# A transformer block on one core: differential queries and keys projected with the tokens stationary, attention pieces and transposing moves at other places

## Chip, cores and metric

One NeuronCore of a Trainium2 chip runs the whole program. The metric is the device time of one execution in microseconds, taken as the median of several runs. A profile of one execution lies beside it; its own time differs a little from the median.

## What is computed

The input is 256 tokens of width 2048 in fp32. Two blocks follow each other: one with sliding-window attention, then one with two attention branches (MLA and differential) whose results are gated and added, and a feed-forward network (FFN). The change lies mostly in the differential branch. Of its projection `dq` and `dk` are 2048 wide each: 8 heads, in each of them two queries and two keys of 128.

```python
S, D, HEADS, HEAD_DIM = 256, 2048, 8, 128

def diff_branch(dq, dk, dv, lq1, lk1, lq2, lk2, sub_g, lambda_init, slopes):
    q = dq.reshape(b, s, DIFF_HEADS, 2, DIFF_HEAD_DIM)
    k = dk.reshape(b, s, DIFF_HEADS, 2, DIFF_HEAD_DIM)
    v = dv.reshape(b, s, DIFF_HEADS, DIFF_V)
    ...
        sc = jnp.einsum('bqhmd,bkhmd->bhmqk', qb, k).astype(jnp.float32) * scale
        sc = sc + alibi[None, :, None]
        sc = jnp.where(chunk_allowed(q_pos, k_pos)[None, None], sc, NEG_INF)
        p = jax.nn.softmax(sc, axis=-1)
        a = (p[:, :, 0] - lam * p[:, :, 1]).astype(v.dtype)
        return jnp.einsum('bhqk,bkhd->bqhd', a, v)
    ...
    o = rmsnorm_2(o, sub_g) * (1.0 - lambda_init)

def second_block(x, ...):
        h = rmsnorm_2(x, attn_norm_g[i])
        c_q, c_kv, k_pe, dq, dk, dv, gate_logits = jnp.split(h @ w_in[i], split_at, axis=-1)
        y_mla = mla_branch(...)
        y_diff = diff_branch(dq, dk, dv, ...)
        g = jax.nn.sigmoid(gate_logits + b_gate[i]).reshape(b, s, 2, d)
        merged = g[:, :, 0] * (y_mla @ w_mla_proj[i]) + g[:, :, 1] * (y_diff @ w_diff_proj[i])
        x = x + merged @ w_out[i]
        h2 = rmsnorm_2(x, ffn_norm_g[i])
        x = x + (jax.nn.silu(h2 @ w_ffn_gate[i]) * (h2 @ w_ffn_up[i])) @ w_ffn_down[i]
    return rmsnorm_2(x, final_norm_g)
```

## The kernel before

**Weights.** All projections together are 5440 weight tiles of 128x128 fp32, used once each. `W.load` (L54) fetches them in chunks of 16 tiles (1 MB) on SP's queue into four buffers `w_raw`. `W.cut` halves a chunk into two cuts of 8 tiles: ACT casts a cut to `w_hi` (L85, rounded fp32), DVE subtracts to `w_lo` (L86); four cuts are held. With activations split in the same way, each tile costs three products.

**Two forms of a projection.** `gemm` holds the weight tile stationary and moves the activations (features on partitions in the result): per tile one matmul with 512 columns (`w_hi` with both parts of the activations) and one with 256 (`w_lo` with the high part). `gemm_nat` holds 128 tokens stationary and moves four weight tiles at once: per four tiles six matmuls with 512 columns, results with tokens on partitions. A strip is 512 columns of output, 64 tiles. `gemm_nats` runs several strips half by half: the first `late` rows of tiles of each, then the rest of each; before, the out projection and the first two strips of the FFN use it.

**Turning.** A result with tokens on partitions is turned by `turned` (L456): DVE transposes it in 32x32 blocks, and `moved` (L444) issues 16 small DMAs that put the blocks where they belong. All 16 go to one queue, POOL's if nothing else is said, or every fourth to another (`fourth`).

**What sets the order.** The projections are written one after another; attention and turning are generators that `between` steps after every few tiles (8 in this stretch, 16 later), at most `apart` ticks from each other; `yield n` in one means that it goes on n ticks later. `between.drain()` finishes what is left. Each engine executes its instructions in order, so a waiting instruction holds up everything behind it on its engine, casts of weights and loads among them.

**The stretch that changes.** For u = 0..3 (two heads each) the main loop projects 4 feature blocks of `dq` and 4 of `dk` with `gemm` (ACT copies half of PSUM to `qk_d`, L417; DVE adds the other half and multiplies, L212), then a strip `dv` with `gemm_nat` (`v_hi`, L984), then queues `attend_d` (L914): `probs_d` for two heads (scores, softmax), `turned_probs` (L462, every fourth move on SP), `values_d` (L885: `a_hi` at L889 needs the turned probabilities), `turned_values` (L903), and the output's split. In u = 0 follow four gates, the MLA projections, and `turn_residual` (L961), which turns the residual stream to `x1n`, 128 moves, all on SP. After the loop come four more gates, a drain, four strips of the diff projection whose merged results are turned, then the out projection and the FFN, whose products are turned and split by `split_turned` (L471: waits 5 ticks, then ACT's `t_hi` at L480). Block 2's MLA heads run as `attend_m` (L787).

## Time and profile before

| | us |
|---|---|
| median of 3 runs | 1979.8 |
| lowest, highest | 1979.0, 1981.18 |
| the profiled execution | 1978.53 |
| its span, first to last instruction | 1976.8 |
| TensorE (PE) busy in it | 1961.3 |
| VectorE (DVE) / ScalarE (ACT) / GpSimd (POOL) busy | 1246.6 / 1000.3 / 524.8 |

PE is TensorE, SP the engine that issues loads. Durations below are of the profiled execution. Instructions on PE overlap at their ends, so a matmul's listed duration is longer than the distance to the next one's start; the distance is what counts.

### The profile page before, as it was taken

Reading aid. Unit: us, or ns where it says so; the run is one execution under the profiler, and the core shown is the slowest. Engines: PE = TensorE matmul, PEld = TensorE weight load, DVE = VectorE, ACT = ScalarE, POOL = GpSimd, SP = SyncE. Lnnn points to the kernel's source line nnn. Section 1 sums busy time; section 2 is a strip of 40 time slices with the busy share of each in tenths; the row PEclk is TensorE's granted clock in tenths of the full one; section 3 lists DMA queues with packets and bytes.
Section 4 is the critical chain, followed back from the end, with each engine's and each line's share of the span. In section 5 each row is a group of like instructions: output and inputs, shape, how many; then the busy total and the mean of one; then the engine's idle time right before and its main releaser. Section 6 shows DMA issues by size and latency. Waiting matters only on the chain. (4 is left out here: it accounts for less than half of the span.)

```text
span 1976.8 us, 27209 instructions
## 1 busy us (share of the span) xinstructions
PE 1961.3 (99%) x9756; PEld 1648.6 (83%) x9756; DVE 1246.6 (63%) x1960; ACT 1000.3 (51%) x1580; POOL 524.8 (27%) x1067
## 2 busy tenths in 40 slices
PE   9999999999999999999999999999999999999998
PEld 8888888888888888888888888887888888888887
DVE  7889766888856655566666666655555555545553
ACT  6677664755645444455554444544444444444443
POOL 0555200022401300013143575433444333330000
PEclk9999999999999999999999999999999999999999
DMA  8565554455555555555556665655656556565553
GB/s 304 186 210 192 187 208 164 171 177 175 174 187 195 173 220 226 198 182 181 204 202 228 212 216 186 241 204 199 207 206 206 204 208 210 206 226 192 192 191 107
DMA packets 100793, 393.16 MB, mean 199 GB/s; under 512 B 27248, under 2 KB 53104, under 8 KB 57520
## 3 DMA queue, kind: packets, MB, share of 16 engines
q1 hardware_dynamic: 65184, 366.17, 52.1%
q0 software_dynamic: 34320, 23.27, 4.2%
q10 hardware_dynamic: 1152, 1.97, 0.3%
q8 instruction: 77, 1.26, 0.3%
q14 instruction: 60, 0.49, 0.1%
HBM read 364.03 MB, written 2.10 MB: 185 GB/s over the span
## 5 line engine op out<-in xcount | busy, mean ns | idle before, releaser
L86 DVE TENSOR_TENSOR w_lo<-w_raw,w_hi 128x1024 fp32r<-128x1024 f32 (+1 forms) x677 | 820.8, 1217 | 555.6 <-ACT w_hi L85 550.7
L85 ACT CAST w_hi<-w_raw 128x1024 fp32r<-128x1024 f32 (+1 forms) x677 | 706.6, 1048 | 699.4 <-PE ps_g L209 632.1
L209 PE MATMUL ps_g<-w_lo,t_hi 128*128 128x512 f32 x1176 | 457.6, 389 | 0.8 <-DVE w_lo L86 0.8
L209 PE MATMUL ps_g<-w_hi,t_hi 128*128 128x512 f32 x1176 | 457.6, 389 | 0.3 <-ACT w_hi L85 0.3
L209 PE MATMUL ps_g<-w_hi,t_lo 128*128 128x512 f32 x1176 | 457.3, 389 | 0.0
L452 POOL DMA_DIRECT2D turned<-turn x576 | 281.7, 497 | 393.2 <-DVE turn L459 169.6
L209 PE MATMUL ps_g<-h,w_hi 128*128 128x512 f32 x1160 | 283.7, 393 | 1.9 <-ACT w_hi L85 1.8
L452 POOL DMA_DIRECT2D prob_t<-prob_tr x336 | 164.5, 498 | 400.6 <-DVE prob_tr L467 249.6
L209 PEld LDWEIGHTS ps_g<-w_lo,t_hi 128*128 128x128 f32 x1176 | 220.7, 188 | 47.0 <-DVE w_lo L86 1.1
L209 PEld LDWEIGHTS ps_g<-w_hi,t_hi 128*128 128x128 f32 x1176 | 220.7, 188 | 46.7 <-ACT w_hi L85 0.7
L209 PEld LDWEIGHTS ps_g<-w_hi,t_lo 128*128 128x128 f32 x1176 | 220.7, 188 | 45.6
L209 PEld LDWEIGHTS ps_g<-h,w_hi 128*128 128x128 f32 x1160 | 212.0, 188 | 46.6 <-issue 2.7
L209 PE MATMUL ps_g<-w_hi,h 128*128 128x512 f32 x768 | 240.9, 391 | 0.0
L209 PEld LDWEIGHTS ps_g<-w_hi,h 128*128 128x128 f32 x768 | 144.2, 188 | 29.8
L209 PEld LDWEIGHTS ps_g<-h,w_lo 128*128 128x128 f32 x1160 | 150.2, 191 | 9.9 <-issue 3.0
L209 PE MATMUL ps_g<-h,w_lo 128*128 128x256 f32 x1160 | 155.1, 284 | 0.0
L209 PE MATMUL ps_g<-w_lo,h 128*128 128x512 f32 x384 | 149.7, 390 | 0.8 <-DVE w_lo L86 0.8
L290 POOL TENSOR_TENSOR rstd<-ms,mhalf 128x2 f32<-128x2 f32 (+1 forms) x10 | 8.4, 837 | 354.5 <-DVE ms L285 338.8
L209 PEld LDWEIGHTS ps_g<-w_lo,h 128*128 128x128 f32 x384 | 72.1, 188 | 16.2 <-DVE w_lo L86 1.6
L452 POOL DMA_DIRECT2D o_t<-o_tr x128 | 62.8, 498 | 63.5 <-issue 24.9
L209 PE MATMUL ps_g<-w_hi,y_m 128*128 128x512 f32 x256 | 79.5, 389 | 0.0
L209 PE MATMUL ps_g<-w_hi,y_d 128*128 128x512 f32 x256 | 79.0, 389 | 0.0
(242 smaller groups left out, 1800.8 us busy)
## 6 DMA issues: line engine op xcount, KB each, us to landing
w_raw<-w SPq DMA_DIRECT2D x337, 1024.0 KB, 5.0
turned<-turn POOLq DMA_DIRECT2D x576, 16.0 KB, 3.9
prob_t<-prob_tr POOLq DMA_DIRECT2D x336, 24.0 KB, 3.6
row<-rw POOLq DMA_DIRECT2D x12, 256.0 KB, 4.0
prob_t<-prob_tr SPq DMA_DIRECT2D x112, 24.0 KB, 2.9
w_raw<-w SPq DMA_DIRECT2D x5, 512.0 KB, 7.5
x1n<-turn SPq DMA_DIRECT2D x128, 16.0 KB, 1.8
o_t<-o_tr POOLq DMA_DIRECT2D x128, 16.0 KB, 3.9
```

The source lines that it names most:

```text
L85: a = nc.scalar.copy(out=hi[:, q], in_=src[:, q])
L86: b = nc.vector.tensor_tensor(out=lo[:, q], in0=src[:, q], in1=hi.bitcast(F32)[:, q], op=ALU.subtract)
L209: nc.tensor.matmul(out=o, lhsT=a, rhs=b, start=start, stop=stop, skip_group_check=True)
L290: nc.gpsimd.tensor_tensor(out=r, in0=t, in1=mhalf[:, 0:n], op=ALU.pow)
L452: (fourth if fourth and a == 3 else queue).dma_start(out=o[32 * b:32 * b + 32, a * n:a * n + n], in_=tr[32 * a:32 * a + 32, b * n:b * n + n])
```

## The change

The differential queries and keys are projected with `gemm_nat` (the columns of their weights are permuted for it): per u two strips of 64 tiles, each with two results of 128 tokens x 512 features. ACT scales each result out of PSUM (L992), and each is turned, 12 moves on POOL and 4 on SP. A new `dense_d`, the first piece of `attend_d`, copies the turned tiles to dense queries and keys on ACT, because the turned layout is not contiguous. `attend_d` is queued before `dv` for u > 0 and begins 14 ticks later, its other pieces at 1, 2, 11, 1, 1, 13, 2 ticks behind each other; `attend_m` begins 2 ticks later. The moves of `turned_values`, of the merged strips, of the FFN's products and of `x1n` are shared 12 to POOL, 4 to SP. The gates' rows are loaded on SP. Gate 4 stands between `dqk` and `dv` of u = 3, gates 5 to 7 after the loop. The first two diff strips run half by half with `gemm_nats`, which ticks until the activation tiles exist; the drain comes behind them. The FFN's products are split 7 ticks after they are moved.

```diff
--- before.py
+++ after.py
@@ -406,6 +406,8 @@
         for ks in (range(late), range(late, n)):
             for col, pp in zip(cols, banks):
                 for k in ks:
+                    while acts[k] is None:
+                        between.tick()
                     hi, lo = W.take(name, k * P, col, 4)
                     for tb in range(2):
                         nat3(pp[tb], acts[k], tb, hi, lo, k == 0, k == n - 1)
@@ -420,14 +422,6 @@
     def scaled(o, ps, rb):
         total(o, ps)
         tt(o, o, rb, ALU.mult)
-    def scores(parts, ps):
-        n = len(parts)
-        for j, (q, k) in enumerate(parts):
-            mm(ps[:, 0:P], q[:, 0:P], k[:, 0:P], j == 0, False)
-        for j, (q, k) in enumerate(parts):
-            mm(ps[:, P:384], q[:, P:S], k[:, 0:S], False, j == n - 1)
     def exps(ps, table, scale, negmax, sums, init, rows=None):
@@ -453,11 +447,11 @@
                     out=o[32 * b:32 * b + 32, a * n:a * n + n], in_=tr[32 * a:32 * a + 32, b * n:b * n + n])
         return o
-    def turned(z, queue=nc.gpsimd):
+    def turned(z, queue=nc.gpsimd, fourth=None):
         tr = unit("turn")
         nc.vector.transpose(out=tr, in_=z)
-        return moved(tr, unit("turned"), queue)
+        return moved(tr, unit("turned"), queue, fourth)
     def turned_probs(p):
@@ -468,9 +462,9 @@
         d = moved(tr, wide("prob_t"), fourth=nc.sync).rearrange("p (a e k i) -> p e k a i", a=4, e=2, k=3)
         return [d[:, e] for e in range(2)]
-    def split_turned(acts, k0, parts):
-        yield 5
+    def split_turned(acts, k0, parts, wait=5):
+        yield wait
         hls = []
         for t in parts:
             t = t.rearrange("p (a g i) -> p g a i", a=4, g=4)
@@ -786,6 +780,7 @@
     def attend_m(j, qn, qr, kn, v):
+        yield 2
         while j // 2 not in roped:
             yield
         negmax, sums, rec = sm("negmax"), sm("sums"), sm("rec")
@@ -864,7 +859,21 @@
     tab_d = unit("tab_d")[:, 0:384]
     nc.scalar.dma_start(out=tab_d, in_=cst[:, C_DD:C_DD + 384])
-    def probs_d(head, q, k):
+    def dense_d(q, k):
+        qs, ks = [], [unit("k_d") for _ in range(2)]
+        for tb in range(2):
+            t = unit("q_d")
+            nc.scalar.copy(out=t.rearrange("p (g a i) -> p g a i", a=4, g=4),
+                           in_=q[tb].rearrange("p (a g i) -> p g a i", a=4, g=4))
+            qs.append(t)
+            for e in range(2):
+                nc.scalar.copy(out=ks[e].rearrange("p (g t a i) -> p t g a i", g=2, t=2, a=4)[:, tb],
+                               in_=k[tb].rearrange("p (a g i) -> p g a i", a=4, g=4)[:, 2 * e:2 * e + 2])
+        return qs, ks
+    def probs_d(head, e, qs, ks):
         negmax, sums, rec = sm("negmax"), sm("sums"), sm("rec")
         slope = 2.0 ** -(head + 1)
         bias = unit("bias")[:, 0:384]
@@ -872,7 +881,9 @@
         p = []
         for m in range(2):
             ps = bank("s")
-            scores([(half(q, m), half(k, m))], ps)
+            qm = [q[:, (2 * e + m) * P:(2 * e + m) * P + P] for q in qs]
+            mm(ps[:, 0:P], qm[0], ks[e][:, m * S:m * S + P], True, False)
+            mm(ps[:, P:384], qm[1], half(ks[e], m), False, True)
             p.append(exps(ps, bias, scale_d, negmax[:, 2 * m:2 * m + 2], sums[:, 2 * m:2 * m + 2], BIG))
         nc.vector.reciprocal(out=rec, in_=sums)
         nc.vector.tensor_scalar(out=rec[:, 2:4], in0=rec[:, 2:4], scalar1=neglam, scalar2=None, op0=ALU.mult)
@@ -909,26 +920,29 @@
             nc.vector.tensor_scalar(out=half(o, qb), in0=half(o, qb), scalar1=r[:, qb:qb + 1], scalar2=None,
                                     op0=ALU.mult)
             nc.vector.transpose(out=to[:, qb], in_=half(o, qb).rearrange("p (d b j) -> p d b j", d=2, b=4))
-        return moved(tr, unit("o_t"))
-    def attend_d(u, q, k, v):
+        return moved(tr, unit("o_t"), fourth=nc.sync)
+    def attend_d(u, q, k, v, wait):
         heads = (2 * u, 2 * u + 1)
+        yield wait
+        qs, ks = dense_d(q, k)
+        yield 1
         p = []
         for e, head in enumerate(heads):
-            p.append(probs_d(head, q[e], k[e]))
-            yield
+            p.append(probs_d(head, e, qs, ks))
+            yield 2 - e
         pts = turned_probs(p)
-        yield 9
+        yield 11
         ms = sm("ms_d")
         os = []
         for e in range(2):
             os.append(values_d(pts[e], [(half(a, e), half(b, e)) for a, b in v], ms[:, 2 * e:2 * e + 2]))
-            yield
+            yield 1
         r = rstd(ms, S)
-        yield
+        yield 1
         ots = [turned_values(o, r[:, 2 * e:2 * e + 2]) for e, o in enumerate(os)]
         for e, head in enumerate(heads):
-            yield 8
+            yield 2 if e else 13
             ot = ots[e].rearrange("p (a d q i) -> p d q a i", a=4, d=2, q=2)
             for d in range(2):
                 y = unit(f"y_d{2 * head + d}", F32R)
@@ -942,7 +956,7 @@
     def gate(i):
-        b = row(R_GATE, i)
+        b = row(R_GATE, i, nc.sync)
         o = []
         for tb, ps in enumerate(gemm_nat("gate", i * 512, h)):
             t = unit("gate")
@@ -966,19 +980,23 @@
                     nc.vector.transpose(
                         out=tr.rearrange("p (a m j) -> p a m j", a=4, m=4)[:, :, i, :],
                         in_=x1[4 * cb + i][:, tb * P:tb * P + P].rearrange("p (a j) -> p a j", a=4))
-                x1n.append(moved(tr, unit("x1n"), nc.sync))
-    mer = []
+                x1n.append(moved(tr, unit("x1n"), fourth=nc.sync))
+    mer, gates = [], []
     for u in range(4):
         qk = []
         for c in (0, 16):
-            for i in range(4):
-                ps = gemm("dqk", c + 4 * u + i, h)
-                if i % 2 == 0:
-                    qk.append(unit("qk_d"))
-                scaled(half(qk[-1], i), ps, rb_2)
+            parts = []
+            for tb, ps in enumerate(gemm_nat("dqk", (c + 4 * u) * P, h)):
+                z = unit("qk_d")
+                nc.scalar.activation(out=z, in_=ps, func=AF.Copy, scale=r_2[:, tb:tb + 1])
+                parts.append(turned(z, fourth=nc.sync))
+            qk.append(parts)
+        v = []
+        if u:
+            between.add(attend_d(u, qk[0], qk[1], v, 14))
+        gates.extend(gate(i) for i in ((), (), (), (4,))[u])
         pp = gemm_nat("dv", u * 512, h)
-        v = []
         for tb in range(2):
             vh, vl = unit("v_hi", F32R), unit("v_lo", F32R)
             nc.scalar.activation(out=vh, in_=pp[tb], func=AF.Copy, scale=r_2[:, tb:tb + 1])
@@ -988,28 +1006,34 @@
         if u == 0:
             between.drain()
             between.every, between.apart = 8, 3
-        between.add(attend_d(u, qk[0:2], qk[2:4], v))
-        if u == 0:
+            between.add(attend_d(u, qk[0], qk[1], v, 6))
             between.add(turn_residual())
             for i in range(4):
                 mer.append(gate(i))
                 for t, ps in zip(mer[i], gemm_nat("mla", i * 512, y_m)):
                     gated(t, ps)
-    gates = [gate(4 + i) for i in range(4)]
+    gates.extend(gate(i) for i in (5, 6, 7))
+    mg = [None] * KD
+    def merge(i, pp):
+        parts = []
+        for tb, ps in enumerate(pp):
+            t = gates[i][tb]
+            gated(t, ps)
+            tt(t, t, mer[i][tb], ALU.add)
+            parts.append(turned(t, fourth=nc.sync))
+        between.add(split_turned(mg, 4 * i, parts))
+    pairs = gemm_nats("diff", [0, 512], y_d, 8)
     between.drain()
     g_ffn = [row(R_FFN, cb, nc.sync) for cb in range(4)]
     between.every, between.apart = 16, 1
-    mg = [None] * KD
-    for i in range(4):
-        parts = []
-        for tb, ps in enumerate(gemm_nat("diff", i * 512, y_d)):
-            t = gates[i][tb]
-            gated(t, ps)
-            tt(t, t, mer[i][tb], ALU.add)
-            parts.append(turned(t))
-        between.add(split_turned(mg, 4 * i, parts))
+    for i, pp in enumerate(pairs):
+        merge(i, pp)
+    for i in (2, 3):
+        merge(i, gemm_nat("diff", i * 512, y_d))
     sums3 = sm("sums3", 8)
@@ -1058,8 +1082,8 @@
             pu = gemm_nat("ffn", DFF + u * 512, h)
         for tb, ps in enumerate(pu):
             tt(parts[tb], ps, parts[tb], ALU.mult)
-            parts[tb] = turned(parts[tb])
-        between.add(split_turned(act, 4 * u, parts))
+            parts[tb] = turned(parts[tb], fourth=nc.sync)
+        between.add(split_turned(act, 4 * u, parts, 7))
     tot = sm("tot", 10)
     fgt = []
@@ -1174,7 +1198,7 @@
         "out_a": i["w_out_a"][0][pairs],
         "in_2": in_2[:, :1280],
         "kpe": np.concatenate([kpe, kpe], axis=1),
-        "dqk": in_2[:, 1344:5440],
+        "dqk": in_2[:, 1344:5440][:, _quarters(2 * D)],
         "dv": in_2[:, 5440:7488],
         "gate": in_2[:, 7488:][:, _quarters(2 * D)],
         "uq": np.concatenate([uq[:, :, :128].reshape(768, -1), uq[:, :, 128:].reshape(768, -1)], axis=1),
```

SP around `turn_residual`, with the u = 1 projection next to it; `w_raw<-w` is a weight chunk, `x1n<-turn` a move of the residual, `row<-rw` a gate's row. Before:

```order
L54 DMA w_raw<-w 128x2048 x6
L452 DMA x1n<-turn 32x128 x32
L54 DMA w_raw<-w 128x2048 x7
L452 DMA x1n<-turn 32x128 x32
L54 DMA w_raw<-w 128x2048 x18
```

and now:

```order
L54 DMA w_raw<-w 128x2048 x6
L446 DMA x1n<-turn 32x128 x4
L484 DMA row<-rw 128x512
L54 DMA w_raw<-w 128x2048
L446 DMA x1n<-turn 32x128 x4
L54 DMA w_raw<-w 128x2048 x7
L446 DMA x1n<-turn 32x128 x8
L54 DMA w_raw<-w 128x2048 x7
L446 DMA turned<-turn 32x128 x4
```

Blocks of 32 moves between weight chunks have become blocks of 4 and 8.

POOL from the values of u = 0 to the probabilities of u = 2; `turned` are here the queries and keys, `prob_t` the turned probabilities, `o_t` the turned values. Before:

```order
L452 DMA o_t<-o_tr 32x128 x32
L490 DMA row<-rw 128x512 x2
L452 DMA prob_t<-prob_tr 32x192 x12
L290 TENSOR_TENSOR rstd<-ms,mhalf 128x4
L452 DMA o_t<-o_tr 32x128 x32
L452 DMA prob_t<-prob_tr 32x192 x12
```

and now:

```order
L446 DMA o_t<-o_tr 32x128 x24
L446 DMA x1n<-turn 32x128 x72
L446 DMA turned<-turn 32x128 x72
L446 DMA prob_t<-prob_tr 32x192 x12
L446 DMA turned<-turn 32x128 x24
L290 TENSOR_TENSOR rstd<-ms,mhalf 128x4
L446 DMA o_t<-o_tr 32x128 x24
L446 DMA turned<-turn 32x128 x24
L446 DMA prob_t<-prob_tr 32x192 x12
```

The moves of `x1n` and of the queries and keys are new in this queue, the values' moves are fewer, and the probabilities stand behind queries' moves and no longer behind the values'.

ACT in the FFN, at its second product; `t_hi` is the split of a turned product, `ffn` the activation of the next strip. Before:

```order
L1055 ACTIVATE ffn<-ps_g,r_12217 128x512 x2
L85 CAST w_hi<-w_raw 128x1024 x13
L480 CAST t_hi<-turned 128x512
L85 CAST w_hi<-w_raw 128x1024 x3
L480 CAST t_hi<-turned 128x512
L1055 ACTIVATE ffn<-ps_g,r_12217 128x512 x2
```

and now:

```order
L1079 ACTIVATE ffn<-ps_g,r_12209 128x512 x2
L85 CAST w_hi<-w_raw 128x1024 x12
L474 CAST t_hi<-turned 128x512
L85 CAST w_hi<-w_raw 128x1024 x2
L474 CAST t_hi<-turned 128x512
L85 CAST w_hi<-w_raw 128x1024 x2
L1079 ACTIVATE ffn<-ps_g,r_12209 128x512 x2
```

The first split stands one cast earlier, the second two, and two casts follow it ahead of the activation.

## Rows read from the trace of the kernel before

**Rows 1.** The page's first part: busy time, share of the span and instructions of each engine.

```profile
PE 1961.3 (99%) x9756; PEld 1648.6 (83%) x9756; DVE 1246.6 (63%) x1960; ACT 1000.3 (51%) x1580; POOL 524.8 (27%) x1067
```

**Rows 2.** What PE waited for over the whole span: us in total, times, longest us.

```profile
PE ps_g L209 <- ACT w_hi L85: 2.1, 2, 1.8
PE ps_g L209 <- DVE w_lo L86: 1.9, 4, 0.8
...
PE ps_s L209 <- DVE q_n L212: 0.9, 1, 0.9
```

**Rows 3.** Windows of the span: a strip of 64 tiles with the tokens stationary, the projection of queries and keys of u = 1 (128 tiles), two FFN strips. Columns: window, us, busy us of PE, weight loads, DVE, ACT, POOL with the number of instructions, granted clock, DMA share, GB/s.

```profile
683.30:705.06 21.76, 21.76 (x97) 18.02 (x96) 10.54 (x11) 8.33 (x8) 0.54 (x1) 1.00 0.67 236
...
770.85:817.45 46.60, 44.83 (x258) 39.27 (x256) 27.03 (x33) 19.60 (x24) 0.00 (x0) 1.00 0.69 259
...
1395.00:1438.52 43.52, 43.52 (x193) 36.04 (x192) 23.12 (x22) 19.17 (x21) 15.80 (x34) 1.00 0.58 205
```

**Rows 4.** Timeline of PE in the projection of queries and keys of u = 1: start, us, instructions; the `w_lo` matmuls of two groups of 16 tiles, five groups apart.

```profile
785.86 2.08 PE L209 MATMUL ps_g<-h,w_lo 128*128 128x256 f32 x16
...
813.69 2.08 PE L209 MATMUL ps_g<-h,w_lo 128*128 128x256 f32 x16
```

**Rows 5.** Timeline of PE at four of its waits: start, us, instructions, idle time before and what ended it.

```profile
456.34 0.38 PE L209 MATMUL ps_s<-k_n,q_n 128*128 128x128 f32 x1 [0.86 <-DVE q_n L212]
...
737.47 0.61 PE L209 MATMUL ps_g<-w_hi,h 128*128 128x512 f32 x2
738.30 0.50 PE L209 MATMUL ps_g<-w_lo,h 128*128 128x512 f32 x1 [0.21 <-DVE w_lo L86]
...
1021.99 0.61 PE L209 MATMUL ps_g<-w_hi,h 128*128 128x512 f32 x2
1023.17 0.50 PE L209 MATMUL ps_g<-w_lo,h 128*128 128x512 f32 x1 [0.57 <-DVE w_lo L86]
1023.50 0.40 PE L209 MATMUL ps_g<-w_hi,h 128*128 128x512 f32 x1
...
1365.05 0.39 PE L209 MATMUL ps_g<-w_hi,t_lo 128*128 128x512 f32 x1
1365.76 0.50 PE L209 MATMUL ps_g<-w_hi,t_hi 128*128 128x512 f32 x1 [0.32 <-ACT w_hi L85]
1367.02 0.50 PE L209 MATMUL ps_g<-w_lo,t_hi 128*128 128x512 f32 x1 [0.76 <-DVE w_lo L86]
```

**Rows 6.** Timeline of SP's queue around `turn_residual`: start, us, what it issued.

```profile
709.80 20.89 SPq L452 DMA_DIRECT2D x1n<-turn  x32
730.79 15.72 SPq L54 DMA_DIRECT2D w_raw<-w  x7
751.02 20.98 SPq L452 DMA_DIRECT2D x1n<-turn  x32
772.10 8.94 SPq L54 DMA_DIRECT2D w_raw<-w  x5
```

**Rows 7.** Timeline of ACT at the waits that precede those of PE.

```profile
735.93 2.00 ACT L85 CAST w_hi<-w_raw 128x1024 fp32r<-128x1024 f32 x2 [7.86 <-DMA w_raw<-w]
...
777.25 2.00 ACT L85 CAST w_hi<-w_raw 128x1024 fp32r<-128x1024 f32 x2 [10.59 <-DMA w_raw<-w]
...
1020.39 0.51 ACT L889 CAST a_hi<-prob_t 128x384 fp32r<-128x384 f32 x1 [7.75 <-DMA row<-rw]
...
1353.95 0.62 ACT L480 CAST t_hi<-turned 128x512 fp32r<-128x512 f32 x1 [6.46 <-DMA turned<-turn]
...
1362.98 0.62 ACT L480 CAST t_hi<-turned 128x512 fp32r<-128x512 f32 x1 [5.56 <-DMA turned<-turn]
```

**Rows 8.** Timeline of POOL: the moves of the values and probabilities ahead of the wait at 1022 us, and the first and last group of the FFN's 32 moves ahead of that at 1365 us.

```profile
988.77 5.88 POOL L452 DMA_DIRECT2D o_t<-o_tr  x12 [11.73 <-DVE rec L878]
...
1008.98 3.91 POOL L452 DMA_DIRECT2D prob_t<-prob_tr  x8 [1.87 <-DMA o_t<-o_tr]
...
1337.50 1.96 POOL L452 DMA_DIRECT2D turned<-turn  x4 [23.62 <-ACT w_hi L85]
...
1354.21 4.40 POOL L452 DMA_DIRECT2D turned<-turn  x9 [1.18 <-DMA turned<-turn]
```

**Rows 9.** Groups of instructions with their shapes, from 770 to 1075 us (u = 1 to 3): count, busy us, mean ns of one, idle time before.

```profile
L212 DVE TENSOR_TENSOR qk_d<-qk_d,rb_kr 128x256 f32<-128x256 f32 x24 | 10.1, 423 | 0.7
L212 DVE TENSOR_TENSOR qk_d<-qk_d,ps_g 128x256 f32<-128x256 f32 x24 | 10.0, 419 | 26.9 <-ACT qk_d L417 26.9
L417 ACT COPY qk_d<-ps_g 128x256 f32<-128x256 f32 x24 | 8.9, 370 | 43.8 <-PE ps_g L209 43.8
...
L984 ACT ACTIVATE v_hi<-ps_g,r 128x512 fp32r<-128x512 f32 x6 | 4.1, 690 | 3.0 <-PE ps_g L209 3.0
```

**Rows 10.** The same view of the FFN's beginning, 1280 to 1420 us.

```profile
L459 DVE STREAM_TRANSPOSE turn<-ffn 128x512 f32<-128x512 f32 x6 | 4.2, 701 | 0.0
...
L480 ACT CAST t_hi<-turned 128x512 fp32r<-128x512 f32 x6 | 3.7, 620 | 18.7 <-DMA turned<-turn 18.7
```

**Rows 11.** DMA issues: queue, count, KB of each, median us from issue to landing.

```profile
turned<-turn POOLq DMA_DIRECT2D x576, 16.0 KB, 3.9
...
x1n<-turn SPq DMA_DIRECT2D x128, 16.0 KB, 1.8
```

**Rows 12.** The stretch of u = 1 to 3 as one window; columns as in rows 3.

```profile
770.85:1074.23 303.38, 301.04 (x1543) 257.73 (x1542) 190.50 (x301) 152.85 (x253) 69.98 (x139) 1.00 0.58 205
```

## Prediction

> **What bounds the kernel now.** I read the busy shares first: PE works 1961.3 us, 99% of the span, and no other engine more than 63% [rows 1]. So the time changes by two things only: what PE is given to do, and how long it stands. The list of PE's waits tells how little is left of the second: 2.1 us for ACT's casts, 1.9 us for DVE's `w_lo`, 0.9 us for `q_n` [rows 2]. The windows come next, because PE's price of a tile is in them: a strip of 64 tiles with the tokens stationary takes 21.76 us, two take 43.52 us, both at full granted clock, whereas the 128 tiles of queries and keys take 46.60 us [rows 3]. Then I followed each wait of PE in its timeline [rows 5] back to the engine and the queue that it came from [rows 6 to 8]. A gain must be in these two places; work on ACT, DVE and POOL is free as long as nobody in PE's line waits for it.
>
> **Step 1, PE's own work.** A strip of 64 tiles is 96 matmuls with 512 columns: 21.76 / 96 = 226.7 ns each, 340 ns a tile. In the old form the `w_lo` groups of five times 16 tiles start at 785.86 and 813.69 [rows 4]: 27.83 / 5 = 5.566 us for 16 tiles, 348 ns a tile. (16 matmuls of 512 are 3.63 us of that, so one of 256 columns costs 121 ns, more than half of a wide one. That surplus is what the new form avoids.) The 128 tiles of one u take 8 x 5.566 = 44.53 us now and 43.52 us after: 1.01 us, four times: **-4.0 us**. The score matmuls keep their number and shapes. A rule of the Trainium skill speaks against this step: "TensorE: Matmul & The Clock Gate", Back-to-back issue gap, gives N/2.4 + 2.5 ns for an isolated matmul, by which both forms come to about 325 ns a tile; it is a rival below.
>
> **Step 2, the waits that go.** (a) In before, SP issues the `x1n` moves in blocks of 32, which take 20.89 and 20.98 us, and the weight chunks queue behind them [rows 6]. ACT waits 7.86 and 10.59 us for `w_raw` [rows 7]. For PE the first costs 738.30 - 737.47 - 2 x 0.227 = 0.38, with 0.10 of restart (after a wait the next distance is 0.33 instead of 0.227, as at 1023.17 [rows 5]) 0.48 us; the second 46.60 - 44.53 = 2.07 us [rows 3, 4]. Now SP has at most 8 moves in a row there, 8 x 0.65 = 5.2 us, half of ACT's shorter wait, which cost 0.48. I take both as gone: -2.55 us. (b) At 1022 us ACT's `a_hi` waits 7.75 us for probabilities [rows 7] that stand on POOL behind 32 moves of values: these begin at 988.77, the probabilities' first move at 1008.98 [rows 8]. PE pays 1023.17 - 1021.99 - 0.454 + 0.10 = 0.83 us [rows 5]. The order now has queries' moves there instead (step 4). -0.83 us. From this I read ACT's cover too: 7.75 - 0.83, **6.9 us of waiting on ACT cost PE nothing**. (c) At 1365 us PE loses (1365.76 - 1365.05 - 0.227) + (1367.02 - 1365.76 - 0.227) + 0.10 = 1.61 us [rows 5], because ACT's two `t_hi` wait 6.46 and 5.56 us [rows 7] for 32 POOL moves, from 1337.50 to 1358.61, 0.66 us a move [rows 8], plus 3.9 us to land [rows 11]. With 24 moves the last lands 8 x 0.66 = 5.3 us sooner. But the second `t_hi` now stands two casts earlier, and a cast (8 tiles) is 21.76 / 8 = 2.72 us of PE, so its wait begins up to 5.4 us sooner and stays about as long; it simply ends sooner, with two casts to catch up on. So -1.61 us if ACT catches up, 0 if not; I take the gain, because ACT does a cast in 1 us [rows 7] where PE needs 2.72. (d) At 456 us PE's scores wait 0.86 us for `q_n` [rows 5]; two ticks of delay for `attend_m` are several times that: -0.9 us. Together 0.48 + 2.07 + 0.83 + 1.61 + 0.9 = **-5.9 us**.
>
> **Step 3, work that lies beside PE.** Off ACT go 32 copies of 370 ns, off DVE 64 operations of some 420 ns [rows 9]: 11.8 and 26.9 us. ACT gets 16 scalings (as `v_hi`, 690 ns [rows 9]) and 24 copies in `dense_d`, 8 of 128x512 and 16 of 128x256; the nearest rows are `t_hi`, 620 ns [rows 10], and the old copy, 370 ns [rows 9]: 11.0 + 5.0 + 5.9 = 21.9 us. DVE gets 16 transposes of 701 ns [rows 10], 11.2 us. Over 175 us of these projections that is +10 us on ACT, -16 us on DVE. ACT has 19.6 busy us in 46.6, DVE 27.0 [rows 3]: 0 on PE, with the casts' waits as the place where it would show. If a dense copy reads its strided tile twice as slowly, 11 us more over four u still lie in ACT's idle time.
>
> **Step 4, the new hand-offs.** They are not in the trace; I bound them. A pair of turned queries must be moved and landed before ACT reaches `dense_d`: 12 moves x 0.66 + 3.9 = 11.8 us for one tile, 19.7 us for two. In ACT's order eight or more casts (21.8 us) lie between the scaling and the copies, so these fit, if POOL is free. Is it? In u = 1 to 3 POOL issues 139 instructions in 303 us, 70 us busy [rows 12]; the change adds 144 moves of queries and keys and most of the 96 of `x1n`, less 24 of values. At 0.66 us that is at most (139 + 216) x 0.66 = 234 of 303 us: room, but not much. The tight place is u = 1's probabilities behind u = 2's queries: 24 + 12 moves x 0.66 + 3.9 = 27.7 us from the first scaling, where ACT's order leaves ten casts, 27.2 us. Past by 0.5 us, with 6.9 us of cover. The lower bound of all these hand-offs is 0 (cover holds); the upper, if each of two per u costs PE what the one at 1022 us did, 8 x 0.83 = 6.6 us. I take **+0.8 us**, one such wait, nearer the lower end, because the only place found short is short by 0.5 us.
>
> **The rest.** `gemm_nats` for two diff strips gives the last pieces of attention 32 more tiles of cover; PE has no wait of its own at the drain [rows 2], so 0. The gates' rows on SP cost one issue each, 0. Gate 4 is the same strip at another place, 0.
>
> **The sum.** -4.0 - 5.9 + 0.8 = -9.1 us against the profiled execution: 1978.53 - 9.1 = 1969.4. The median of the runs lies 1.27 us above that execution, so in its terms 1970.7 us, 0.46% less.
>
> **Rivals.** *The hand-offs eat the gain.* With the upper bound of step 4: 1979.8 - 9.9 + 6.6 = 1976.5 us, no change that a measurement of this kernel can tell (about 0.2%, 4 us). For it: ACT executes in order and now waits for moved tiles at 12 more places; against: the 6.9 us of cover.
> *The FFN wait stays.* Step 2(c) fails, since the splits stand earlier while their data come sooner by the same 5.3 us, and a little more is lost at the next strips: 1970.7 + 1.6 = 1972.3, up to 1974.
> *The two forms cost PE the same.* If distances were proportional to columns, 16 tiles would be 16 x (226.7 + 113.3) = 5.44 us, as in the new form, and step 1 would be 0: 1974.7. The rows contradict it: 5.566 was measured over 80 tiles. By the skill's rule above the gain would be about 0.5 us, an estimate, near this case; the measured 226.7 and 121 ns lie above both its figures, and the trace does not agree with it.
> *POOL becomes the bound, slower.* If POOL's order in the run puts another 24 moves ahead of the probabilities of u = 1, 2 and 3 (the values' block, for instance, that before stood there), each waits 24 x 0.66 = 15.8 us longer. At 0.5 us past already and with 6.9 us of cover PE loses 9.4 us each time: 1979.8 - 9.9 + 28 = 1998 us. It decides from 10 moves on, and the kernel is slower than before once the three lose 10 us together, at 15 moves. Against it: the printed order has the values behind the queries.
> *The change does less than it says.* If loads still stood behind moves on SP, 2.55 us would stay: 1973.3. The order shows no such block.
>
> **Chances.** Forecast 0.60; hand-offs 0.14; FFN wait 0.12; equal forms 0.04; POOL, slower 0.06; less than it says 0.04. Below 1975.8 is faster by over 0.2%, above 1983.8 slower: faster 0.80, same 0.14, slower 0.06. The range: below, all of step 2 and no new wait, and another 2 to 3 us of small waits that I do not see singly, some 1967; above, the hand-offs at their upper bound, 1977. About 2 in 10 stay outside.
>
> **What will show it.** Right: the query and key strips take 21.76 us each at full clock; no block of 32 moves on SP, no wait of ACT for `w_raw` of 8 to 10 us; nothing of PE's waits at the four places; PE's busy time down by some 4 us; ACT's waits for `k_d`, `q_d` or `a_hi` shorter than 6.9 us. Wrong: PE waiting at its scores, or for `w_hi` behind a copy in `dense_d`; POOL's moves end to end through u = 1 to 3; PE's busy time unchanged, which would fell step 1.

## The result and the profile after

| | before | after |
|---|---|---|
| median of the runs, us | 1979.8 | 1969.61 |
| lowest, highest | 1978.44, 1982.5 | 1968.55, 1971.06 |
| the profiled execution, us | 1978.53 | 1970.1 |
| its span | 1976.8 | 1968.3 |

The ratio of after to before is 0.9944, 95% interval 0.9934 to 0.9955: faster by 0.45 to 0.66%. Forecast were 1970.7 us and 0.46%. The page's first part, to set beside [rows 1], shows PE busy for 4.3 us less and ACT for 10.7 us more:

```profile
PE 1957.0 (99%) x9500; PEld 1635.9 (83%) x9500; DVE 1232.6 (63%) x1912; ACT 1011.0 (51%) x1588; POOL 587.4 (30%) x1195
```

The two strips of u = 1 as windows (columns as in [rows 3]) take 43.52 us together, where the old form took 46.60 with a wait in it:

```profile
768.17:789.93 21.76, 21.76 (x97) 18.02 (x96) 10.79 (x10) 8.92 (x9) 0.00 (x0) 1.00 0.53 193
789.93:811.69 21.76, 21.76 (x97) 18.02 (x96) 11.13 (x10) 9.70 (x11) 11.74 (x24) 1.00 0.66 217
```

SP's queue around `turn_residual`, to set beside [rows 6], has no block of 32 moves, and the loads of weights stand between short ones:

```profile
706.12 2.41 SPq L446 DMA_DIRECT2D x1n<-turn  x4
...
711.72 2.42 SPq L446 DMA_DIRECT2D x1n<-turn  x4
716.31 32.97 SPq L54 DMA_DIRECT2D w_raw<-w  x7
```

The list of PE's waits, to set beside [rows 2], has lost `q_n` and the casts. Of the two waits left for `w_lo`, the one at 417 us (0.37 us) was there before, with 0.36 us; the other is new:

```profile
PE ps_g L209 <- DVE w_lo L86: 1.1, 2, 0.8
...
PE ps_g L209 <- DVE h L249: 0.3, 1, 0.3
```

PE's timeline puts the new one at 1262 us, in the FFN's first strips, where the kernel before had no wait. The distance from 1262.21 to 1263.47 is 1.26 instead of 0.23 us; with the 0.2 ahead of it and the restart behind it PE loses 1.3 us:

```profile
1261.79 0.39 PE L209 MATMUL ps_g<-w_hi,t_lo 128*128 128x512 f32 x1
1262.21 0.50 PE L209 MATMUL ps_g<-w_hi,t_hi 128*128 128x512 f32 x1
1263.47 0.50 PE L209 MATMUL ps_g<-w_lo,t_hi 128*128 128x512 f32 x1 [0.76 <-DVE w_lo L86]
```

ACT's timeline leads to it: `t_hi` of the out projection's last turned residual waits 7.32 us, with casts behind it.

```profile
1250.74 0.62 ACT L474 CAST t_hi<-turned 128x512 fp32r<-128x512 f32 x1 [3.42 <-DMA turned<-turn]
...
1260.59 0.62 ACT L474 CAST t_hi<-turned 128x512 fp32r<-128x512 f32 x1 [7.32 <-DMA turned<-turn]
```

POOL's and SP's timelines lead on: POOL stands for 2.66 us within the residual's moves and issues the last of them at 1256.25, just after SP's first weight chunk at 1256.11.

```profile
1220.87 6.83 POOL L446 DMA_DIRECT2D turned<-turn  x14 [2.66 <-issue]
...
1248.44 8.31 POOL L446 DMA_DIRECT2D turned<-turn  x17 [1.47 <-DMA turned<-turn]
```

```profile
1245.98 10.02 SPq L446 DMA_DIRECT2D turned<-turn  x16
1256.11 27.23 SPq L54 DMA_DIRECT2D w_raw<-w  x7
```

That last move is the longest of the view by tile for 1254 to 1262 us: 4.3 us to land where the median is 2.0.

```profile
DMA to landing us min/median/max: 1.6/2.0/4.3
```

By stages of the weights that PE works on, the span changed thus: MLA with the projections of u = 0, -2.3 us (398 to 659 us); the gates and the MLA output, -0.5; u = 1 to 3, 303.38 to 297.64, -5.7; the diff strips 0; out and FFN, 801.50 to 801.55, 0. The last is a loss of 1.6 us avoided at 1365 us and others of 1.3 at 1262 and 0.2 at 1252 us taken. The window of u = 1 to 3, to set beside [rows 12]:

```profile
768.17:1065.81 297.64, 297.64 (x1351) 247.94 (x1350) 178.30 (x264) 160.41 (x258) 126.59 (x255) 1.00 0.61 207
```

### The profile page after: what moved, and what is told of

It reads as the page before. It is cut to its first block, busy times and chain, and to the rows that moved or that the text cites. A ratio compares the mean times of both kernels' runs of the same rounds, so it can differ in the third digit from the quotient of the medians.

```text
span 1968.3 us, 27377 instructions
## 1 busy us (share of the span) xinstructions
PE 1957.0 (99%) x9500; PEld 1635.9 (83%) x9500; DVE 1232.6 (63%) x1912; ACT 1011.0 (51%) x1588; POOL 587.4 (30%) x1195
## 4 chain that ended last, share of the span: by engine, by line
PE 97%; DVE 1%; SPq 0%; ACT 0%; DMA 0%; issue 0%; POOL 0%; POOLq 0%; ACTq 0%
PE ps_g L209 91%; PE ps_s L209 4%; PE ps_t L209 2%; SPq L446 0%; DVE w_lo L86 0%; PE ps_warm L230 0%; DMA w_raw<-w 0%; DVE rope_t L212 0%; ACT w_hi L85 0%; DVE k_n L212 0%; POOL rstd L290 0%; ACT x1n L1145 0%; DVE q_r L212 0%; DVE y L686 0%; DVE y L685 0%
## 5 line engine op out<-in xcount | busy, mean ns | idle before, releaser
L446 POOL DMA_DIRECT2D turned<-turn x648 | 317.1, 497 | 549.2 <-DVE turn L453 267.0
L209 PE MATMUL ps_g<-w_hi,h 128*128 128x512 f32 x1280 | 400.7, 391 | 0.0
L209 PEld LDWEIGHTS ps_g<-w_hi,h 128*128 128x128 f32 x1280 | 240.3, 188 | 50.5 <-issue 0.3
L209 PE MATMUL ps_g<-w_lo,h 128*128 128x512 f32 x640 | 249.1, 389 | 0.0
L209 PE MATMUL ps_g<-h,w_hi 128*128 128x512 f32 x648 | 160.1, 394 | 0.0
L209 PEld LDWEIGHTS ps_g<-w_lo,h 128*128 128x128 f32 x640 | 120.2, 188 | 24.6
L209 PEld LDWEIGHTS ps_g<-h,w_hi 128*128 128x128 f32 x648 | 117.9, 188 | 25.5 <-issue 2.3
L209 PEld LDWEIGHTS ps_g<-h,w_lo 128*128 128x128 f32 x648 | 84.7, 191 | 7.3 <-issue 2.7
L209 PE MATMUL ps_g<-h,w_lo 128*128 128x256 f32 x648 | 88.3, 284 | 0.0
L446 POOL DMA_DIRECT2D x1n<-turn x96 | 47.0, 497 | 100.7 <-DVE turn L980 42.3
```

Source lines behind the costliest of these rows:

```text
L209: nc.tensor.matmul(out=o, lhsT=a, rhs=b, start=start, stop=stop, skip_group_check=True)
L446: (fourth if fourth and a == 3 else queue).dma_start(out=o[32 * b:32 * b + 32, a * n:a * n + n], in_=tr[32 * a:32 * a + 32, b * n:b * n + n])
```

## Experiments

In every kernel that has "small moves", they write a tile that nobody reads; nothing of the computation is left out in any.

**1. The pause of POOL by count.** Counted over all of POOL's moves, the pause at 1220.87 us follows its 854th, and others follow the 128th, 249th, and so on, every 121 moves in both kernels, whatever is moved.

```diff
+    dump = const.tile([P, 128], F32, name="dump")
+    for i in range(58):
+        r, c = 32 * (i % 4), 4 * (i // 4 % 32)
+        nc.gpsimd.dma_start(out=dump[r:r + 32, c:c + 4], in_=q_o[15][1][r:r + 32, c:c + 4])
```

> The changed kernel with 58 more small moves (32 x 4 values, into a tile that nobody reads) on POOL's queue at about 220 us, where POOL is idle. Theory (a pause by count): in both traces POOL stands for 2.2 to 2.9 us after every 121st move (the 854th in the changed kernel is followed by 2.66 us at 1218 us, in the moves of the out projection's residual), and that pause makes the new wait of PE at 1262 us (1.42 us). With 58 more, the pauses come 58 moves earlier in the later work: in the last merged strip and in the FFN's first product. PE's wait at 1262 us goes, time -1.4 us, unless the pause in the FFN's first product costs PE something (ACT's wait there grows from 4.4 to at most 7.1 us, near the 6.9 us of cover: 0 to 0.3 us). Rival (the residual's own 96 moves and its 32 moves on SP make the wait): it stays at 1.4 us, time unchanged.

Measured: 1970.75 us, ratio to before 0.9949 (0.9936 to 0.9961). The pauses still follow the 854th and the 975th move and so on, which are now moves of the last merged strip and of the FFN's first product; POOL's timeline:

```profile
1161.11 4.88 POOL L446 DMA_DIRECT2D turned<-turn  x10 [2.77 <-issue]
```

PE's wait at 1262 us is gone, but the time did not fall: the theory missed. Of the 1.5 us that PE no longer loses at 1252 and 1262 us, 0.8 came back, 0.36 at 1181 and 0.45 at 1304 us. And in the profiled execution the granted clock was lower (0.90, where the changed kernel's has 1.00) in the window from 320 to 336 us; it was 0.50, the lower of its two levels, from 333 to 336 us, after PE had run the small matmuls of the residual's norm and stood for 0.56 us. By the start of the next stage that cost 0.9 us. The changed kernel has the same matmuls and 0.63 us of standing there without the fall; experiments 2 and 6 have the fall too. Besides, 1.3 us is within what the intervals leave open.

```profile
320.00:336.00 16.00, 15.44 (x101) 14.17 (x100) 5.63 (x15) 3.65 (x10) 0.71 (x1) 0.90 0.34 114
```

**2. The control with 121.** The same, `range(121)`.

> As the run with 58 more moves, but with 121. Theory (a pause by count): the pauses of the later work fall on the same moves as in the changed kernel, so PE's wait at 1262 us stays at 1.4 us and the time is that of the changed kernel within 0.2 us. Rival (anything else that more moves on POOL do, a shift of when things land for example): it differs from the changed kernel as the run with 58 does, in the same direction.

Measured: 1971.29 us, 0.9955 (0.9941 to 0.9968). The pause fell on the same move as in the changed kernel:

```profile
1221.88 7.82 POOL L446 DMA_DIRECT2D turned<-turn  x16 [2.76 <-issue]
```

but PE did not wait at 1262 us. So the pause alone does not make that wait; my theory fell in this form. What differs is the end of the chain: POOL issued the last move at 1257.51, ahead of SP's chunk at 1258.32, and it landed in 1.65 us. Instead PE lost 1.7 us at 644 us, where ACT's `a_hi` of u = 0 waits for probabilities behind moves of `x1n` on POOL. In the changed kernel the same wait of ACT is 6.70 us and costs PE nothing; here it is 8.62. The changed kernel, then experiment 2:

```profile
640.64 0.51 ACT L900 CAST a_hi<-prob_t 128x384 fp32r<-128x384 f32 x1 [6.70 <-DMA x1n<-turn]
...
643.11 0.51 ACT L904 CAST a_hi<-prob_t 128x384 fp32r<-128x384 f32 x1 [8.62 <-DMA x1n<-turn]
```

**3. The pause out of the FFN's second product, in the kernel before.** The small moves of experiment 1 with `range(93)`.

> The kernel before with 93 more small moves on POOL at about 220 us. In the kernel before a pause (the 733rd move, 2.71 us at 1339.5 us) falls into the 32 moves of the FFN's second product, ahead of PE's wait of 1.61 us at 1365 us. With 93 more the pauses come 28 moves later: this one at the boundary to the third product. Theory (the pause makes that wait): the 32 moves take 18.4 instead of 21.1 us, ACT's second t_hi waits 2.9 instead of 5.6 us, and PE's 1.61 us go. Rival (as the prediction has it, 32 moves at 0.66 us are too many): the wait stays above 1 us. The pause before (the 612th) moves 28 later too, into the middle of the residual's moves at some 1230 us, and may cost PE up to 1.4 us near 1270 us; so the verdict is in PE's rows at 1365 us, not in the total, which I expect between -1.6 and 0 us.

Measured: 1981.58 us, 1.0005 (0.9996 to 1.0014). The 32 moves took 19.8 instead of 21.1 us, and PE lost 0.9 instead of 1.6 us, at 1371 us:

```profile
1371.84 0.50 PE L209 MATMUL ps_g<-w_lo,t_hi 128*128 128x512 f32 x1 [0.61 <-DVE w_lo L86]
```

Without the pause a little under half of that wait went, so neither the theory nor the rival held. ACT's second `t_hi` waited 6.58 us, not the 2.9 that I expected; its first waited 2.39 instead of 6.46. Experiment 7 shows what the number of moves is worth. The pause is now in the residual's moves, at 1232 us, and PE lost 1.2 us at 1262 and 2.2 around 1274 us.

**4. `x1n` alone, in the kernel before.**

```diff
-                x1n.append(moved(tr, unit("x1n"), nc.sync))
+                x1n.append(moved(tr, unit("x1n"), fourth=nc.sync))
```

The kernel has the small moves of experiment 1 besides, with `range(25)`.

> The kernel before with one part of the change alone: of x1n's moves 12 go to POOL and 4 to SP, as in the changed kernel (and 25 more small moves on POOL at 220 us, so that with the 96 of x1n it is 121 more and later pauses of POOL fall where they fell). Theory: the waits at 738 and 776 us go, -2.5 us, and nothing else changes, 1977.3 us against 1979.8. Rival (another load is late in their place, or POOL's moves of the values queue behind x1n's 96): less than 1 us gained.

Measured: 1976.93 us, 0.9979 (0.9971 to 0.9988). Both waits are gone: the gate's strip takes 21.76 us and the projection of u = 1 takes 44.53. The gain, 1.2 to 2.9 per mille, is 2.4 to 5.7 us, the forecast 2.5 at its lower end. Experiments 3, 6 and 7, which keep the old queue of `x1n`, show why: ACT's wait there is not the same in each execution. After the 7.86 us of [rows 7] it was in 7, 6 and 3, in this order:

```profile
737.10 1.99 ACT L85 CAST w_hi<-w_raw 128x1024 fp32r<-128x1024 f32 x2 [9.19 <-DMA w_raw<-w]
```

```profile
737.58 1.99 ACT L85 CAST w_hi<-w_raw 128x1024 fp32r<-128x1024 f32 x2 [9.68 <-DMA w_raw<-w]
```

```profile
738.13 1.99 ACT L85 CAST w_hi<-w_raw 128x1024 fp32r<-128x1024 f32 x2 [10.10 <-DMA w_raw<-w]
```

and the strip took 22.27, 23.59, 24.09 and 24.49 us, that is 0.5, 1.8, 2.3 and 2.7 more than 21.76. The difference between ACT's wait and PE's loss is 7.35 to 7.37 us in all four. This is the cover, the waiting on ACT that costs PE nothing; past it each further microsecond of ACT's wait adds one of PE's.

**5. The old form of the projection, in the changed kernel.**

```diff
-            for tb, ps in enumerate(gemm_nat("dqk", (c + 4 * u) * P, h)):
-                ...
-                parts.append(turned(z, fourth=nc.sync))
+            for i in range(4):
+                ps = gemm("dqk", c + 4 * u + i, h)
+                if i % 2 == 0:
+                    qk.append(unit("qk_d"))
+                scaled(half(qk[-1], i), ps, rb_2)
```

The scores and the columns of the weights are put back to match, the dense copies go, and the small moves of experiment 1 are there with `range(71)`.

> The changed kernel with its queries and keys projected in the old form again (features on partitions, no turning, no dense copies; all other parts of the change stay; 71 more small moves on POOL at 220 us, so that with the 192 fewer moves of queries and keys the count is 121 less and later pauses fall on the same moves). Theory (prediction, step 1): each of the four projections takes 44.5 us and not 43.5, +4.0 us, 1973.6 us against the changed kernel's 1969.6, and the new hand-offs (step 4) cost nothing, so that nothing else changes. Rival (both forms cost PE the same, and the gain is the waits alone): 1969.6 to 1970. Second rival (the hand-offs cost the changed kernel something, 0.8 us as predicted or more): the old form is slower by less than 4 us, since those waits go with it.

Measured: 1975.49 us, 0.9968 (0.9956 to 0.9981), against the changed kernel's 0.9944. The projection of u = 1 as a window, columns as in [rows 3]:

```profile
768.68:813.21 44.53, 44.53 (x258) 39.35 (x256) 27.15 (x36) 18.77 (x23) 5.87 (x12) 1.00 0.56 193
```

From 512 us to the diff strips it is slower by 3.6 us (557.19 against 553.54): the form's 4.0 less some tenths. The profiled span is 4.9 us longer; 1.6 of that are in out and FFN, since the wait near 1262 us is 2.3 us here. The rival of equal forms is out.

**6. `attend_m` two ticks later, alone, in the kernel before.**

```diff
     def attend_m(j, qn, qr, kn, v):
+        yield 2
         while j // 2 not in roped:
```

> The kernel before with attend_m beginning two ticks later, alone. Theory (prediction, step 2d): PE's wait for q_n at 455 us goes, and the small ones next to it: -0.9 to -1.6 us in the stretch from 398 to 515 us. Rival (the wait moves to another head or to the probabilities): less than 0.3 us gained in that stretch. The total is 1979 us, hardly told from 1980 by time; the verdict is in PE's waits.

Measured: 1979.39 us, 0.9986 (0.9977 to 0.9994). No wait for `q_n` is in PE's list, and from 398 to 616 us PE needs 216.33 instead of 217.88 us: 1.6 us, since two waits of 0.28 us each at 421 and 457 us went with the one of 1.03. The windows before and in this run, columns as in [rows 3]:

```profile
397.94:615.82 217.88, 216.53 (x1175) 183.19 (x1174) 165.90 (x366) 123.44 (x245) 52.06 (x106) 1.00 0.52 174
...
399.31:615.64 216.33, 215.98 (x1175) 183.32 (x1174) 165.91 (x366) 123.05 (x245) 52.59 (x107) 1.00 0.51 176
```

**7. The FFN's moves alone, in the kernel before.**

```diff
-            parts[tb] = turned(parts[tb])
+            parts[tb] = turned(parts[tb], fourth=nc.sync)
```

`turned` passes `fourth` on, as in the changed kernel.

> The kernel before with the FFN's products moved 12 on POOL and 4 on SP, alone (the split stays 5 ticks behind). The pause of POOL after its 733rd move still falls into the second product, but there are 24 moves instead of 32. Theory (prediction, step 2c: the number of moves makes the wait at 1365 us): it goes, PE's 1.6 us are gained. Rival (the pause makes it): PE still loses 0.8 us or more there.

Measured: 1979.32 us, 0.9989 (0.9980 to 0.9998). PE does not wait at 1365 us, although the pause is in the product's moves and ACT's wait is a microsecond longer than the 5.56 us of [rows 7]:

```profile
1347.08 3.92 POOL L452 DMA_DIRECT2D turned<-turn  x8 [2.37 <-issue]
```

```profile
1358.48 0.62 ACT L480 CAST t_hi<-turned 128x512 fp32r<-128x512 f32 x1 [6.56 <-DMA turned<-turn]
```

It ends 4.5 us sooner than before, at 1358.48 instead of 1362.98 us, with two casts behind it to catch up on.

**8. The attention 6 ticks behind.**

```diff
-            between.add(attend_d(u, qk[0], qk[1], v, 14))
+            between.add(attend_d(u, qk[0], qk[1], v, 6))
```

> The changed kernel with attend_d beginning 6 ticks behind instead of 14 for u = 1 to 3: the dense copies stand one to two casts behind the last scaling on ACT, where the changed kernel has nine. Theory (prediction, step 4): ACT must wait for the moves, 0.7 + 12 x 0.66 + 3.9 = 12.5 us from the scaling, less two to four casts' time: 7 to 10 us each time; past the cover of 6.9 us PE loses 1 to 4 us per u, +3 to +9 us in all. Rival (the cover is larger than 6.9 us, or the copies wait less): within 0.5 us of the changed kernel.

Measured: 1971.68 us, 0.9950 (0.9938 to 0.9963); no difference from the changed kernel. I had misjudged how far the copies move: in the trace ACT waits for them in u = 1 alone, and below the cover:

```profile
823.25 0.71 ACT L872 COPY k_d<-turned 128x256 f32<-128x256 f32 x2 [2.11 <-DMA turned<-turn]
...
833.30 0.71 ACT L872 COPY k_d<-turned 128x256 f32<-128x256 f32 x2 [6.50 <-DMA turned<-turn]
```

From 768 us to the diff strips PE needs 297.91 instead of 297.64 us. So 6.5 us of waiting cost at most 0.3, which agrees with a cover near 7 us, but what happens past it in this place was not tried.

**9. The three parts on waits together, in the kernel before.** The edits of experiments 4, 6 and 7, with the 25 small moves.

> The kernel before with three parts of the change that concern waits alone, and nothing of the projection's form: x1n's moves 12 on POOL and 4 on SP, attend_m two ticks later, the FFN's products 12 on POOL and 4 on SP (and 25 small moves on POOL at 220 us, so that the pauses fall where they fell). Theory (the terms add up): PE's waits at 455, 738, 776 and 1365 us go, 1.0 + (0.5 to 2.3) + 2.1 + 1.6 = 5.2 to 7.0 us; the wait for the probabilities at 1022 us (0.8 us) stays. Time 1973 to 1975 us against 1980. Rival (one wait gone uncovers the next): less than 4 us.

Measured: 1973.24 us, 0.9963 (0.9949 to 0.9976); span 1971.5, 5.3 us less than before. Of the waits only that for the probabilities of u = 2 is left, 1.0 us at 1018. The terms add up, and what is missing to the changed kernel's 1968.3, 3.2 us, is the form (4.0) and that wait, less the new one at 1262 us.

**10. The drain ahead of the diff strips.**

```diff
-    pairs = gemm_nats("diff", [0, 512], y_d, 8)
     between.drain()
+    pairs = gemm_nats("diff", [0, 512], y_d, 16)
```

> The changed kernel with the drain ahead of the diff strips again and the strips one after another, each whole. Theory (prediction: half by half gives the last attention 32 more tiles of cover): the chain of u = 3 takes 47 ticks, 40 are left after gate 4, dv and gates 5 to 7, and what the drain issues early must still wait for its moves, so the last four of y_d come some 20 us after the strip's start, which needs them after 12 of 16 rows of tiles, 16.3 us: PE waits 1 to 5 us around 1080 us. Rival (as in the kernel before, where no wait stands there): within 0.5 us of the changed kernel.

Measured: 1971.23 us, 0.9950 (0.9938 to 0.9963). The rival was right; the four diff strips as a window:

```profile
1066.11:1153.15 87.04, 87.04 (x386) 72.07 (x384) 55.57 (x65) 39.03 (x46) 35.22 (x72) 1.00 0.64 223
```

Half by half is worth nothing here. My ticks were no measure of when the data come: a drain issues the last pieces at once.

**11. Fewer POOL moves at the residual's end.**

```diff
-            parts.append(turned(z, nc.sync if cb % 2 and tb else nc.gpsimd))
+            parts.append(turned(z, nc.sync if cb % 2 and tb else nc.gpsimd, nc.sync if cb == 3 else None))
```

> The changed kernel with 4 of the 16 POOL moves of the last residual's first tile on SP (SP has then 20 in a row there, POOL 12). Theory (the new wait at 1262 us comes when POOL's last move of the residual is issued behind SP's next weight chunk and lands in 4.3 us instead of 1.6): POOL ends some 2 us sooner, SP's chunk starts 2.5 us later, the last move lands in under 2 us, PE's wait at 1262 us is below 0.3 us, and the time 1 to 1.5 us under the changed kernel's. Rival (the wait is that for SP's moves, which are the later ones now): it stays or grows, up to +2 us.

Measured: 1976.26 us, 0.9975 (0.9966 to 0.9984), slower than the changed kernel. The transfer did what I said: POOL's last move is issued at 1254.84, ahead of SP's chunk at 1256.30, and lands in 1.95 us. But with the other times the order on DVE came out otherwise: the copy of `rstd`, which POOL computes behind its moves, stands ahead of a `t_lo` that PE needs sooner, and PE waits 4.8 us for that.

```profile
1256.11 0.17 DVE L1065 COPY r<-rstd 128x2 f32<-128x2 f32 x1 [7.53 <-POOL rstd L290]
```

```profile
PE ps_g L209 <- DVE t_lo L212: 4.8, 1, 4.8
```

During that standstill the granted clock fell to 0.50, the lower of its two levels, and it stayed there until 1262 us: the matmuls with 512 columns started 0.43 us apart instead of 0.23, which cost another 2.1 us. PE loses 8.2 us here in all, the changed kernel 1.5; the difference of 6.7 us agrees with that of the medians (6.65) and of the spans (6.3). The window behind the standstill:

```profile
1258.00:1262.00 4.00, 3.93 (x9) 3.13 (x10) 1.75 (x3) 0.54 (x1) 0.00 (x0) 0.50 0.96 375
```

**The wait at 1262 us over the traces.** Experiment 11 (-1.46 us, 1.95 us to land) has the other waits told above and stands apart. When POOL's last move of the residual was issued, relative to SP's next weight chunk, and what PE lost behind it:

| kernel | move after (+) or ahead (-) of the chunk, us | it landed in, us | PE lost, us |
|---|---|---|---|
| experiment 3 | +1.51 | 4.2 | 2.2 |
| experiment 5 | +0.83 | 4.9 | 2.3 |
| experiment 10 | +0.41 | 4.8 | 1.9 |
| the changed kernel | +0.14 | 4.3 | 1.3 |
| experiment 8 | +0.03 | 3.8 | 0.9 |
| experiment 9 | -0.23 | 2.0 | 0 |
| experiment 4 | -0.69 | 1.9 | 0 |
| experiment 2 | -0.80 | 1.7 | 0 |
| experiment 6 | -0.93 | 1.6 | 0 |
| experiment 7 | -1.14 | 1.7 | 0 |
| the kernel before | -1.78 | 1.7 | 0 |
| experiment 1 | -1.89 | 1.6 | 0 |

The sign decides in all twelve. In the changed kernel the late move lands at 1260.56 us and ACT's `t_hi` begins at 1260.59, whereas SP's last move had landed at 1257.22, so the wait is for POOL's move and not for SP's. The pause, late in the residual's moves, pushes POOL towards the chunk, and some tenths of a microsecond from one execution to the next do the rest (experiment 2). The weight of each in a single execution was not measured.

## Why the prediction was right, point by point

The span fell by 8.5 us where 9.1 were forecast, and the medians by 10.2.

- **Step 1, PE's own work, -4.0.** Held. 43.52 against 44.53 us in the same place without a wait (experiments 4, 5 and 9); undoing the form alone cost 3.6 us in the stretch. The Trainium skill, "TensorE: Matmul & The Clock Gate", Back-to-back issue gap, has both forms within some 0.6 us of each other per four projections, an estimate by its formula for an isolated matmul; the trace does not agree with it, as [rows 4] and experiment 5 show.
- **Step 2a, `x1n` on SP, -2.55.** The mechanism held (experiment 4). The size was that of one execution, the cheapest of four: the first wait costs 0.5 to 2.7 us. This may be why the medians differ by more than the profiled executions, which no run here shows by itself. One reading was wrong and cost nothing: 5.2 us for 8 moves is half of ACT's longer wait, and two thirds of the shorter. The block of 8 took 5.12 us, and ACT's longest wait for `w_raw` is 2.1 us now.
- **Step 2b, the probabilities behind the values, -0.83.** Held: no `a_hi` waits from 768 us on, and in experiment 9, which keeps the old order, 1.0 us remain. Which part of the new order did it was not tried by itself.
- **Step 2c, the FFN's moves, -1.61.** Held by itself (experiment 7). I had not seen that a pause of POOL, 2.71 us, lies in the 21.1 us of the 32 moves; without it nearly half of PE's loss goes (experiment 3). The 0.66 us a move holds this pause and POOL's waits for moves to land; issued one behind the other they take 0.49 us each [rows 8].
- **Step 2d, `q_n`, -0.9.** Too small: 1.6 us (experiment 6), because I counted the largest of three waits.
- **Step 3, ACT and DVE beside PE, 0.** Held. The dense copies took 619 and 402 ns (620 and 370 assumed), and ACT waited for none.
- **Step 4, new hand-offs, +0.8.** The place that I called tight, the probabilities of u = 1, had no wait. The one that came was the probabilities of u = 0 behind moves of `x1n`: 6.70 us on ACT, 0 on PE, and 1.7 in experiment 2. The cover, taken as 6.9 us everywhere, is 7.0 there (8.62 - 1.67), 7.4 at 738 us, 6.0 at 1262 us (7.32 - 1.33) and 8.5 at 776 us in the old form (10.59 - 2.07; 8.5 again in experiments 3, 6 and 7).
- **Half by half at the drain, 0.** Held (experiment 10).
- **Missed:** +1.5 us at 1252 and 1262 us, in code that the change does not touch. With the form's 3.6 for 4.0, 2d's 1.6 for 0.9 and no hand-off's 0.8, it leaves the sum within a microsecond of the forecast. That these errors cancel so well is luck; the two large terms, the form and the waits, are not. No rival had it: the slower rival put POOL's queue into the attention, and the wait came where POOL's moves meet SP's loads.

## What to carry to other kernels

Where PE is bound, price a wait upstream by its length less the cover of its place, and find the cover from executions that differ: at 738 us it repeated to hundredths while the wait varied by 2.2 us. It differs from place to place, from 6.0 to 8.5 us here. Count moves per queue, but also what the other queue starts meanwhile: POOL's last move landed 2.6 us later behind a weight chunk than ahead of one (4.3 against 1.7 us), as long as POOL takes to issue five moves. An edit that shifts a count or a time can change waits and orders far from it, so read the whole list of waits after, not only the places that were meant.

## What the runs showed of the hardware

POOL's queue stands for 2.2 to 3.0 us, at a few places for up to 4.3, after its 128th move and after each further 121, in every kernel here, with moves of 512 bytes, 16 KB, 24 KB and 256 KB alike. In the changed kernel's timeline of POOL, for example, the 733rd, 975th and 1096th:

```profile
1111.67 4.89 POOL L446 DMA_DIRECT2D turned<-turn  x10 [2.81 <-issue]
...
1383.59 3.90 POOL L446 DMA_DIRECT2D turned<-turn  x8 [2.44 <-issue]
...
1601.21 3.42 POOL L446 DMA_DIRECT2D turned<-turn  x7 [2.22 <-issue]
```

What makes it was not tried.

A move of POOL that is issued while a weight chunk of SP is under way (between its issue and its landing, counted over all of POOL's transfers in a trace) lands in 4.4 us, the median of 851 in the changed kernel, otherwise in 1.7 (330 moves); before, 4.1 (859) and 1.7 (194). DVE's work is not the cause: in the changed kernel the moves behind a chunk take 4.7 us with DVE busy for under 30% of their first 1.6 us and 4.1 with over 70%, the others 1.9 and 1.7. SP's own small moves are slower too: 3.59 us behind a chunk, otherwise 1.95. The Trainium skill, "DMA: Bandwidth & Descriptors", Issuing engines are not separate DMA queues, says that transfers started by different engines run on the same DMA engines and interleave; the longer landings agree with that.
